# Layer 0's modulations through weight slots on TensorE, residuals spread over three feed-forward groups, a third weight slot, final gathers by pairs of tiles

## The chip, the core and the metric

The kernel runs on one core of one Trainium2 chip. The metric is the device time of one execution in microseconds (us). The core has engines that work side by side, each through its own instructions in order: TensorE (PE, matmuls; PEld is its weight load), VectorE (DVE), ScalarE (ACT), GpSimd (POOL) and SyncE (SP), which here issues most DMAs. Data lies in HBM, in SBUF (128 partitions) and, for matmul results, in PSUM. TensorE's clock has two levels, and the profile gives the granted clock as a share of full speed.

## What is computed

The reference is a two-layer network on 512 tokens `x` and 256 context tokens `ctx`, width 1024, all in fp32. Its main loop, cut:

```python
for l in range(DEPTH):                                   # DEPTH = 2
    mod_x = (cond_x @ w_ada[l] + b_ada[l]).reshape(bsz, 6, 1, d)
    mod_c = (cond_c @ w_ada[l] + b_ada[l]).reshape(6, 1, d)
    hx = x * (1.0 + mod_x[:, 1]) + mod_x[:, 0]
    ...
    x = _layer_norm(DEEPNORM_ALPHA * x + mod_x[:, 2] * mix_x, ln_g[l, 0], ln_b[l, 0])
    hx = x * (1.0 + mod_x[:, 4]) + mod_x[:, 3]
    f_x = _channel_mix(hx, l, ...)      # l = 0: SwiGLU, 2816 wide; l = 1: 8 experts, 2 chosen
    x = _layer_norm(DEEPNORM_ALPHA * x + mod_x[:, 5] * f_x, ln_g[l, 1], ln_b[l, 1])
```

`ctx` goes the same way in layer 0 with `mod_c`. The mix is a projection by `w_in`, two recurrent branches in both directions (HGRN2 and mLSTM), gates and a projection by `w_out`. A modulation m of a layer (m = 0 to 5) is thus a row of 1024 numbers for each of the two streams: a product of `cond` (2 by 1024) with 1024 by 1024 of `w_ada`, 4 MB in HBM.

## The kernel before

**Products.** fp32 products are made of three passes (`mm3`, L166 to L168): each operand is split in a high part and the rest. A weight comes by DMA into a raw buffer `wr` (512 KB, two of them); ACT copies it to `wh` (L133, L150) and DVE subtracts into `wl` (L134, L151). A pair `wh`/`wl` of 128x2048 each is a weight slot. There are two, taken in turn by `load_w` and `load_pair`, so one set of weights is prepared while TensorE works on the other. In a steady stretch TensorE never waits.

**Modulations.** Three forms exist. `ada` (L276) multiplies raw `w_ada` by `cond` on TensorE in plain fp32, 2x512 of output, eight matmuls for a half of a modulation; each raw buffer holds two of them. Layer 0 does m = 1 and 0 so at the start and m = 2 in the mix. `ada_vec` multiplies on the vector engines: for each of 8 k it loads 128x1024 of `w_ada` and adds it, scaled by one column of `cond` for each stream, to an accumulator `acc` (L324 and L326 on DVE; with `both=True` the second stream goes over ACT, L320, and POOL, L322). Its `end` splits `acc` (ACT L332, DVE L333) and sums over the partitions by four or eight short matmuls with the constant `esel` (L338). Layer 0 does m = 4 and m = 3 so with `both=True`, from the gates to the middle of `w_out`; m = 5 and the six of layer 1 go by `ada_vec` in the first seven groups of the feed-forward, from `between`. `ada_put` adds the bias and turns the row.

**Stages in the trace (us).** 0 to 47 start and m = 1, 0; 50 to 505 mix of layer 0 (m = 2 at 203 to 252; the last HGRN heads and gates with m = 4 at 390 to 505); 505 to 620 `w_out`, norm and split of the rows (m = 3); 620 to 1225 feed-forward; 1225 to 1590 mix of layer 1; 1590 to 1660 `w_out` and router; 1660 to 2220 experts; 2226 to 2269 last gathers, norm and output.

**Feed-forward (`swiglu`).** Eleven groups of 256 hidden columns; for each, gate and up products block by block (`b`) and, in a block, for the 512 tokens and the 256 of the context (`spans`), then the down product of all six token tiles in two halves, evacuated by `evac` on DVE (L1015). After group `GRES` = 8, DVE multiplies each half by the modulation row `bd` (L1018) and adds the residual (L1019), which `residual` brings from HBM and POOL scales (L909, L910). The last down pass takes two groups.

**End of layer 1.** `finish` normalises rows (POOL's `pow`, L841; DVE L892), writes them to `xhd`; the router runs on DVE; POOL gathers the first experts' tokens (L1203, indirect DMA); SP loads a register with the first expert's number (`TENSOR_LOAD expi`) and then the experts' weights. In the midst of the experts, `rest` loads the rows `xhd` as `xrows` and scales them on POOL by eight 128x1024 operations (L1450, L1451). At the end eight indirect DMAs (L1529) add the experts' results to the four tiles of `xrows`, first j = 0 for all four tiles, then j = 1; each tile is then normed (L831, L838, L841, L1541, L1542) and written.

**Order.** Each engine's order is fixed when the program is built, by a scheduler that goes by priorities and readiness; SP's queue too is in order, so a DMA that waits holds up those behind it.

Of the kernel before, what the change touches and what calls it, by code (L numbers as in the profile page):

```python
# [17 lines left out]
KT = 8  # L18
# [31 lines left out]
class Kern:  # L50
# [47 lines left out]
    def raw(self, w, own=None):  # L98
        if own is not None:
            return own[0].tile([P, 1024], F32, tag="ar", name=self.nm("ar"), bufs=own[1])[:, :w]  # L100
# [4 lines left out]
    def load_w(self, shape, src, scale=None, own=None):  # L105
# [5 lines left out]
        if own is None:  # L111
            wp, wb = self.wps[self.wi % len(self.wps)]
            self.wi += 1
            h, lo = (wp.tile([P, 2048], F32R, tag=x, name=self.nm(x), bufs=wb) for x in ("wh", "wl"))
        else:
            h, lo = (self.ow.tile([P, 1548], F32R, tag="early", name=self.nm("a"), bufs=2) for _ in range(2))
# [3 lines left out]
        for i, j in parts:  # L120
            w = shape[1] * (j - i)
            r = self.raw(w, own)
# [14 lines left out]
    def load_pair(self, n, src):  # L137
# [4 lines left out]
        for k0 in range(0, KT, kp):  # L142
            wp, wb = self.wps[self.wi % len(self.wps)]
            self.wi += 1
            h, lo = (wp.tile([P, 2048], F32R, tag=x, name=self.nm(x), bufs=wb) for x in ("wh", "wl"))
# [132 lines left out]

    def ada_put(self, l, m, half, pr, ns):
# [16 lines left out]
    def ada_vec(self, l, ms, pool, ns=2, both=False, tmp=None):  # L296

# [3 lines left out]
        if isinstance(ms, int):  # L301
            ms = ((ms, 0), (ms, 1))
        w = self.I["w_ada"][l].rearrange("(k p) c -> k p c", p=P)
        c0 = [m * D + half * 512 for m, half in ms]
        acc = [self.ow.tile([P, 1548], F32, tag="early", name=self.nm("acc"), bufs=2) for _ in range(ns)]
        for k in range(KT):
            wk = self.raw(1024, (pool, 2) if pool else None)
            if c0[1] == c0[0] + 512:
                nc.sync.dma_start(wk, w[k][:, c0[0]:c0[0] + D])
            else:  # L310
                for h in range(2):
                    nc.sync.dma_start(wk[:, 512 * h:512 * h + 512], w[k][:, c0[h]:c0[h] + 512])
            for s in range(ns):
                cs = self.cond32[:, k, s:s + 1]
                o = acc[s][:, :D]
                if both and s:
                    for h in range(2):
                        c = slice(512 * h, 512 * h + 512)
                        t = o[:, c] if k == 0 else acc[h][:, D:D + 512]
                        nc.scalar.activation(t, wk[:, c], AF.Copy, scale=cs)  # L320
                        if k:
                            nc.gpsimd.tensor_tensor(o[:, c], o[:, c], t, OP.add)  # L322
                elif k == 0:
                    nc.vector.tensor_scalar(o, wk, cs, None, op0=OP.mult)  # L324
                else:
                    nc.vector.scalar_tensor_tensor(o, wk, cs, o, op0=OP.mult, op1=OP.add)  # L326

        def end():
            for i in range(ns):
                h, lo = ((tmp or self.lp).tile([P, D], F32R, tag="xn", name=self.nm("xn"), bufs=2) for _ in range(2))  # L330
                o = acc[i][:, :D]
                nc.scalar.activation(h, o, AF.Copy)  # L332
                nc.vector.tensor_tensor(lo, o, h.bitcast(F32), OP.subtract)  # L333
                if i == 0:
                    prs = [self.psum("g", [ns, 512]) for _ in range(2)]
# [4 lines left out]
            for (m, half), pr in zip(ms, prs):  # L340
                self.ada_put(l, m, half, pr, ns)
# [1279 lines left out]
```

## Time and profile before

| | |
|---|---|
| median of 3 runs | 2271.22 us (2268.95 to 2277.7) |
| profiled execution | 2271.0 us, of it span 2269.2 us and 1.8 us around it |
| busy in the span | PE 2060.2 us (91%), DVE 1511.8 (67%), ACT 914.4 (40%), POOL 255.6 (11%) |
| instructions | 31798 |
| HBM | 305.98 MB read, 22.09 MB written |

The busy time is a mean over stages. The rows further below are read stage by stage: how long PE is busy in a stretch, at which clock, and what ended the idle time ahead of an instruction. Matmuls are pipelined, so a record's length is longer than what one adds to a dense row of them.

### The profile page before, as it was taken

The page shows a single profiled execution, that of the slowest core. Times are in us where ns is not written, and L with a number is a line of the kernel's source. Part 1 is how long each engine was busy: PE and PEld are TensorE (multiplying, and loading weights), DVE is VectorE, ACT ScalarE, POOL GpSimd, SP SyncE. Part 2 cuts the span into 40 slices and gives each one's busy share as a digit, 9 for nine tenths or more (in the row PEclk, how much of TensorE's full clock was granted, in tenths as well). Part 3 has the DMA queues.
Part 4 walks back from the last instruction along what each step waited for, and adds up shares of the span by engine and source line. Part 5 has one row for each costly group of instructions (what it writes and reads, how often), then busy time and mean ns, then how long its engine had stood idle before and what let it go on. Part 6 is the DMA issues. An engine that isn't in the chain of part 4 may idle for free. (4 is left out here: it accounts for less than half of the span.)

```text
span 2269.2 us, 31798 instructions
## 1 busy us (share of the span) xinstructions
PE 2060.2 (91%) x12225; PEld 1753.9 (77%) x12225; DVE 1511.8 (67%) x2527; ACT 914.4 (40%) x1447; POOL 255.6 (11%) x211
## 2 busy tenths in 40 slices
PE   8999899897899999999699999999869999897991
PEld 4886788896788788888588888899867787675771
DVE  4465776857866774334727577686679768778774
ACT  3345333343432222212124354334247656665661
POOL 1001101414300000000400001111310000004003
PEclk9999999998899999999899999999869999899995
DMA  7122302246543662112222222124368779887875
GB/s 261 40 89 89 93 27 63 63 138 206 192 153 127 197 208 71 56 56 65 84 66 85 58 83 66 47 61 141 135 196 302 255 242 317 269 271 262 289 272 126
DMA packets 231493, 330.21 MB, mean 146 GB/s; under 512 B 14512, under 2 KB 181620, under 8 KB 231336
## 3 DMA queue, kind: packets, MB, share of 16 engines
q1 hardware_dynamic: 227928, 317.04, 43.2%
q0 software_dynamic: 3408, 11.08, 1.9%
q8 instruction: 98, 1.61, 0.3%
q14 instruction: 59, 0.48, 0.1%
HBM read 305.98 MB, written 22.09 MB: 145 GB/s over the span
## 5 line engine op out<-in xcount | busy, mean ns | idle before, releaser
L168 PE MATMUL g<-xh,wl 128*128 128x512 f32 (+1 forms) x1168 | 402.4, 345 | 15.8 <-DVE wl L134 15.8
L166 PE MATMUL g<-xh,wh 128*128 128x512 f32 (+1 forms) x1168 | 402.5, 345 | 2.5 <-ACT wh L133 2.0
L167 PE MATMUL g<-xl,wh 128*128 128x512 f32 (+1 forms) x1168 | 401.8, 344 | 1.9 <-DVE xl L385 1.9
L134 DVE TENSOR_TENSOR wl<-wr,wh 128x1024 fp32r<-128x1024 f32 x240 | 296.2, 1247 | 139.3 <-ACT wh L133 131.1
L133 ACT ACTIVATE wh<-wr 128x1024 fp32r<-128x1024 f32 x240 | 249.3, 1055 | 244.5 <-PE sc L168 72.8
L166 PE MATMUL g<-wh,xh 128*128 128x256 f32 x1024 | 298.2, 292 | 15.0 <-DVE pre L975 6.6
L167 PE MATMUL g<-wl,xh 128*128 128x256 f32 x1024 | 298.8, 292 | 8.4 <-DVE wl L130 5.8
L168 PE MATMUL g<-wh,xl 128*128 128x256 f32 x1024 | 296.8, 290 | 0.0
L168 PEld LDWEIGHTS g<-xh,wl 128*128 128x128 f32 x1168 | 221.4, 190 | 43.6 <-DVE wl L134 17.1
L166 PEld LDWEIGHTS g<-xh,wh 128*128 128x128 f32 x1168 | 221.7, 190 | 30.3 <-ACT wh L133 2.9
L167 PEld LDWEIGHTS g<-xl,wh 128*128 128x128 f32 x1168 | 221.2, 189 | 29.5 <-DVE xl L385 2.4
L151 DVE TENSOR_TENSOR wl<-wr,wh 128x1024 fp32r<-128x1024 f32 x154 | 191.2, 1251 | 50.6 <-ACT wh L150 49.6
L166 PEld LDWEIGHTS g<-wh,xh 128*128 128x128 f32 x1024 | 198.5, 194 | 20.2 <-DVE pre L975 6.9
L167 PEld LDWEIGHTS g<-wl,xh 128*128 128x128 f32 x1024 | 198.4, 194 | 11.8 <-DVE wl L130 8.0
L168 PEld LDWEIGHTS g<-wh,xl 128*128 128x128 f32 x1024 | 198.6, 194 | 0.8 <-issue 0.8
L150 ACT ACTIVATE wh<-wr 128x1024 fp32r<-128x1024 f32 x154 | 161.6, 1056 | 75.8 <-DMA wr<-in_moe_w_gate_up 64.3
L326 DVE SCALAR_TENSOR_TENSOR acc<-ar,cond,acc 128x1024 f32<-128x1024 f32 x77 | 101.3, 1330 | 35.3 <-DMA ar<-in_w_ada 35.3
L864 DVE TENSOR_TENSOR s<-g,s 128x512 f32<-128x512 f32 (+1 forms) x44 | 24.4, 555 | 146.9 <-PE g L168 146.9
L524 POOL TENSOR_TENSOR ss<-ss,mhalf 128x4 f32<-128x4 f32 (+1 forms) x22 | 27.2, 1237 | 666.9 <-DVE ss L523 499.0
L865 ACT ACTIVATE hh<-s 128x512 fp32r<-128x512 f32 (+1 forms) x44 | 23.0, 523 | 174.2 <-DVE s L864 174.2
L467 PE MATMUL sc<-tmp,s 128*128 128x128 f32 x560 | 79.6, 290 | 9.7 <-DVE tmp L475 7.4
L909 POOL TENSOR_TENSOR xr<-xr,gbc 128x512 f32<-128x512 f32 x20 | 31.0, 1552 | 484.1 <-DMA xr<-xd 476.5
(483 smaller groups left out, 4164.7 us busy)
## 6 DMA issues: line engine op xcount, KB each, us to landing
wr<-in_moe_w_gate_up SPq DMA_DIRECT2D x176, 512.0 KB
wr<-in_moe_w_down SPq DMA_DIRECT2D x88, 512.0 KB
wr<-in_w_in SPq DMA_DIRECT2D x64, 512.0 KB
ar<-in_w_ada SPq DMA_DIRECT2D x64, 512.0 KB
wr<-in_ffn_w_gate_up SPq DMA_DIRECT2D x44, 512.0 KB
wr<-in_w_ada SPq DMA_DIRECT2D x32, 512.0 KB
wr<-in_ffn_w_down SPq DMA_DIRECT2D x22, 512.0 KB
wr<-in_w_out SPq DMA_DIRECT2D x16, 512.0 KB
```

The lines of the kernel that those rows point to most:

```text
L133: nc.scalar.activation(fl(h), r, AF.Copy)
L134: nc.vector.tensor_tensor(fl(lo), r, fl(h).bitcast(F32), OP.subtract)
L150: nc.scalar.activation(v(h, u), r, AF.Copy)
L151: nc.vector.tensor_tensor(v(lo, u), r, v(h, u).bitcast(F32), OP.subtract)
L166: nc.tensor.matmul(out, ah, bh, start=(i == 0), stop=False)
L167: nc.tensor.matmul(out, ah, bl, start=False, stop=False)
L168: nc.tensor.matmul(out, al, bh, start=False, stop=(i == n - 1))
L326: nc.vector.scalar_tensor_tensor(o, wk, cs, o, op0=OP.mult, op1=OP.add)
L467: nc.tensor.matmul(pl[:, c - a], kc[:, c * P:(c + 1) * P], apx(qa, c * P + T, [[2 * hh, 64 // hh], [hh - T, 2], [1, hh]]), start=True, sto ...
L524: nc.gpsimd.tensor_tensor(ss[:, :n], ss[:, :n], self.mhalf[:, :n], OP.pow)
L864: nc.vector.tensor_tensor(s, pu, s, OP.mult)
L909: nc.gpsimd.tensor_tensor(xr, xr, gb[0][:, c], OP.mult)
```

## The change

1. `ada_slot` is new: a half of a modulation (2 MB of `w_ada`) is loaded by two 1 MB DMAs straight into a weight slot, `wh` and `wl` both taken as plain fp32 space, and its eight matmuls with `cond` come when the returned `end` is called. Layer 0's m = 2 goes so (one half ahead of each `wq` load), m = 4 (one half in each of the last two gates) and m = 3 (one half in each of the first two quarters of `w_out`, in the third slot).
2. A third weight slot (`wh3`, `wl3`) takes: the two halves of m = 3, the last quarter of layer 0's `w_out`, the loads of `ada_vec` in the feed-forward (m = 5 of layer 0 and layer 1's six; four 1 MB DMAs for a modulation in place of eight of 512 KB, and `h`, `lo` of its end in the slot too), and the first weights of the last down pass.
3. In the feed-forward's first group the 512 tokens of both blocks come ahead of the context's 256.
4. `GRES` becomes a function of the tile: tiles 0, 1 take their residual after group 6, 2, 3 after 7, and 4, 5 after 8; a tile's later down products are multiplied by `bd` one by one. The residual rows are prepared one group ahead.
5. After layer 1's last `pow`, POOL scales `pre` by `ln_g`, `ln_b` (eight 128x1024 operations) and SP writes it to `xd`; `xrows` in the experts is loaded from there and its eight POOL operations go.
6. The final gathers go by pairs of tiles: j = 0 and 1 of tiles 0, 1, then of 2, 3.

```diff
+    def ada_slot(self, l, m, half, third=False):
+        ws = [t.bitcast(F32).rearrange("p (k c) -> p k c", c=512) for t in self.wslot(third)]
+        for i, t in enumerate(ws):
+            nc.sync.dma_start(t, w[:, 4 * i:4 * i + 4, c0:c0 + 512])
+        def end():
+            pr = self.psum("g", [2, 512])
+            for k in range(KT):
+                nc.tensor.matmul(pr, self.cond32[:, k], ws[k // 4][:, k % 4], start=k == 0, stop=k == KT - 1)
+            self.ada_put(l, m, half, pr, 2)
+        return end
...
+    def ada_vec(self, l, m, ns):
+        for k0 in range(0, KT, 4):
+            for i, t in enumerate(self.wslot(True)):
+                wk = t.bitcast(F32).rearrange("p (k c) -> p k c", c=D)
+                k1 = k0 + 2 * i
+                nc.sync.dma_start(wk, w[:, k1:k1 + 2, m * D:m * D + D])
...
-            if pr == 0:
-                if l == 0:
-                    self.ada(0, (2,))
+            if l == 0:
+                end = self.ada_slot(0, 2, pr)
...
             wq = self.w_cols(w, O_HQ + 256 * pr, 256)
+            if l == 0:
+                end()
...
-            if l == 0 and g == 1:
-                self.ends = [self.ada_vec(0, 4, None, both=True)]
+            if l == 0 and g > 1:
+                end = self.ada_slot(0, 4, g - 2)
...
-            for b in range(nb):
-                for t0, n in spans:
+            for b, (t0, n) in ([(b, s) for s in spans for b in range(nb)] if g == 0 else itertools.product(range(nb), spans)):
...
-                dh, dl = self.load_w((nb, D), lambda i, j: dv[:, i:j])
+                dh, dl = self.load_w((nb, D), lambda i, j: dv[:, i:j], third=g == len(groups) - 1 and not ps)
...
-                                  scale=lambda k: self.norm_col(l, k)) for nq in nqs]
+                                  scale=lambda k: self.norm_col(l, k), third=nq == 3 and not last) for nq in nqs]
+                if l == 0 and nqs[0] < 2:
+                    end = self.ada_slot(0, 3, nqs[0], True)
...
             if last:
+                with tc.issue_after(self.pow.ins if hasattr(self.pow, "ins") else self.pow):
+                    for t in range(nt):
+                        for g, op in zip(gn, (OP.mult, OP.add)):
+                            nc.gpsimd.tensor_tensor(pre[:, t], pre[:, t], g, op)
+                        nc.sync.dma_start(self.xd[t * P:(t + 1) * P], pre[:, t])
...
-                if end:
-                    m = self.lp.tile([P, 512], F32, tag="xr", name=self.nm("xm"), bufs=4)
+                if g > GRES(t):
+                    m = self.fp.tile([P, 512], F32, tag="s", name=self.nm("xm"), bufs=2)
                     nc.vector.tensor_tensor(m, p, bd, OP.mult)
                     nc.vector.tensor_tensor(o, o, m, OP.add)
-                    return
-                nc.vector.tensor_tensor(o, p, o, OP.add)
-                if g == GRES:
+                else:
+                    nc.vector.tensor_tensor(o, p, o, OP.add)
+                if g == GRES(t):
                     nc.vector.tensor_tensor(o, o, bd, OP.mult)
-                    nc.vector.tensor_tensor(o, o, self.residual(t, half, gb), OP.add)
+                    nc.vector.tensor_tensor(o, o, res.pop((t, half)), OP.add)
+                if (t, half) == (nt - 1, 1):
+                    for u in tiles:
+                        if GRES(u) == g + 1:
+                            res.update({(u, h): self.residual(u, h, gb) for h in range(2)})
...
-                nc.sync.dma_start(x, xhd.rearrange("(t p) c -> p t c", p=P))
+                nc.sync.dma_start(x, self.xd[0:TX].rearrange("(t p) c -> p t c", p=P))
...
-                for t in range(NX):
-                    nc.gpsimd.tensor_tensor(x[:, t], x[:, t], g1, OP.mult)
-                    nc.gpsimd.tensor_tensor(x[:, t], x[:, t], b1, OP.add)
...
-        for j in range(2):
-            for t in range(NX):
+        for u in range(0, NX, 2):
+            for j, t in itertools.product(range(2), (u, u + 1)):
...
-GRES = D_FF // 256 - 3
+def GRES(t):
+    return D_FF // 256 - 3 - (NT - 1 - t) // 2
```

**Where it moves instructions.** On DVE, in the down pass of group 8 before: `bd` is the modulation row, `xr` a residual, `wl` the next group's weights.

```order
L1015 TENSOR_TENSOR pre_4488<-sc_9159,pre_4488 128x512
L1019 TENSOR_TENSOR pre_4488<-pre_4488,xr_9154 128x512
L1018 TENSOR_TENSOR pre_4488<-pre_4488,bd_5585 128x512
L1015 TENSOR_TENSOR pre_4488<-o_9173,pre_4488 128x512
L1019 TENSOR_TENSOR pre_4488<-pre_4488,xr_9168 128x512
L1018 TENSOR_TENSOR pre_4488<-pre_4488,bd_5585 128x512
L1015 TENSOR_TENSOR pre_4488<-sc_9187,pre_4488 128x512
L1019 TENSOR_TENSOR pre_4488<-pre_4488,xr_9182 128x512
L1018 TENSOR_TENSOR pre_4488<-pre_4488,bd_5585 128x512
L134 TENSOR_TENSOR wl_9202<-wr_9203,wh_9201 128x1024
```

The weights of the next group stand behind all twelve halves, of three operations each. The changed kernel's DVE in the pass of group 7, its middle one:

```order
L1020 TENSOR_TENSOR xm_8576<-sc_8569,bd_5480 128x512
L135 TENSOR_TENSOR wl_8688<-wr_8689,wh_8687 128x1024
L1021 TENSOR_TENSOR pre_4468<-pre_4468,xm_8576 128x512
L1020 TENSOR_TENSOR xm_8586<-o_8579,bd_5480 128x512
L1020 TENSOR_TENSOR xm_8596<-sc_8589,bd_5480 128x512
L1021 TENSOR_TENSOR pre_4468<-pre_4468,xm_8586 128x512
L1021 TENSOR_TENSOR pre_4468<-pre_4468,xm_8596 128x512
L1023 TENSOR_TENSOR pre_4468<-o_8599,pre_4468 128x512
L1023 TENSOR_TENSOR pre_4468<-sc_8609,pre_4468 128x512
L1025 TENSOR_TENSOR pre_4468<-pre_4468,bd_5480 128x512 x2
L1026 TENSOR_TENSOR pre_4468<-pre_4468,xr_8291 128x512
L1026 TENSOR_TENSOR pre_4468<-pre_4468,xr_8295 128x512
```

One quarter of the next weights (`wl_8688`) has moved among the evacuations; the other three stand behind the pass as before.

On POOL, at the end of layer 1's norm, before (`r` is `pow`, `gat` the first experts' gathers):

```order
L841 TENSOR_TENSOR r_13934<-r_13934,mhalf 128x1
L841 TENSOR_TENSOR r_14025<-r_14025,mhalf 128x1
L1203 DMA gat_14217<-xhd,ix_0_14187 128x1024
L1203 DMA gat_14219<-xhd,ix_1_14198 128x1024
L1203 DMA gat_14222<-xhd,ix_0_14209 64x1024
```

and in the changed kernel at the same place:

```order
L843 TENSOR_TENSOR r_13798<-r_13798,mhalf 128x1
L843 TENSOR_TENSOR r_13889<-r_13889,mhalf 128x1
L997 TENSOR_TENSOR pre_13256<-pre_13256,ln_g_1704_13265 128x1024 x2
L997 TENSOR_TENSOR pre_13256<-pre_13256,ln_b_1705_13267 128x1024 x2
L997 TENSOR_TENSOR pre_13256<-pre_13256,ln_g_1704_13265 128x1024
L997 TENSOR_TENSOR pre_13256<-pre_13256,ln_b_1705_13267 128x1024
L997 TENSOR_TENSOR pre_13256<-pre_13256,ln_g_1704_13265 128x1024
L997 TENSOR_TENSOR pre_13256<-pre_13256,ln_b_1705_13267 128x1024
L1215 DMA gat_14093<-xhd,ix_0_14063 128x1024
L1215 DMA gat_14095<-xhd,ix_1_14074 128x1024
L1215 DMA gat_14098<-xhd,ix_0_14085 64x1024
```

Eight 128x1024 operations have come between `pow` and the first gather. SP's queue at the same place, before (`expi` is the first expert's number, `wr` its weights):

```order
L894 DMA xhd<-pre_13398 128x1024 x4
L1428 TENSOR_LOAD expi
L1428 ISA x2
L123 ISA
L123 DMA wr_14500<-in_moe_w_gate_up 128x4x256
```

and in the changed kernel:

```order
L998 DMA xd<-pre_13256 128x1024 x4
L1440 TENSOR_LOAD expi
L1440 ISA x2
L124 ISA
L124 DMA wr_14376<-in_moe_w_gate_up 128x4x256
```

Four writes to `xd`, each behind POOL's operations on its tile, have come between the writes to `xhd` and the register load with the experts' first weights.

## Rows read from the trace of the kernel before

**Rows 1.** The page's first part: TensorE's busy time over the span.

```profile
PE 2060.2 (91%) x12225; PEld 1753.9 (77%) x12225; DVE 1511.8 (67%) x2527; ACT 914.4 (40%) x1447; POOL 255.6 (11%) x211
```

**Rows 2.** Busy time by stretch: columns named in the first line, x = records.

```profile
core 0: us, PE busy (x) PEld busy (x) DVE busy (x) ACT busy (x) POOL busy (x), PEclk, DMA share, GB/s
0.00:50.00 50.00, 41.84 (x152) 16.07 (x153) 20.57 (x61) 14.29 (x30) 6.98 (x23) 0.97 0.79 275
...
203.00:252.00 49.00, 38.94 (x168) 20.81 (x168) 26.22 (x63) 17.73 (x29) 4.34 (x4) 0.86 0.46 139
410.00:460.00 50.00, 40.65 (x309) 38.43 (x308) 48.10 (x55) 22.69 (x41) 25.74 (x18) 0.97 0.29 83
505.00:600.00 95.00, 80.32 (x604) 75.09 (x603) 79.59 (x127) 36.58 (x69) 31.96 (x22) 0.91 0.58 189
600.00:625.00 25.00, 15.13 (x78) 13.04 (x78) 21.41 (x34) 14.65 (x32) 10.83 (x9) 0.73 0.54 189
...
900.00:950.00 50.00, 50.00 (x266) 42.02 (x265) 21.88 (x35) 11.04 (x15) 0.00 (x0) 1.00 0.20 64
1085.00:1118.00 33.00, 14.06 (x47) 10.14 (x46) 29.84 (x27) 1.06 (x1) 24.86 (x16) 0.74 0.25 78
1220.00:1235.00 15.00, 12.04 (x95) 11.04 (x93) 13.49 (x24) 10.98 (x25) 0.55 (x1) 1.00 0.42 108
...
2047.00:2104.00 57.00, 44.46 (x185) 33.26 (x183) 51.69 (x47) 34.09 (x45) 26.32 (x8) 0.97 0.77 253
2104.00:2154.00 50.00, 49.34 (x227) 39.92 (x228) 35.21 (x43) 29.36 (x40) 0.00 (x0) 1.00 0.86 286
```

**Rows 3.** What TensorE waited for: us in total, times, longest.

```profile
PE g L168 <- DVE wl L134: 16.6, 3, 15.4
PE sc L371 <- DVE pre L892: 8.8, 2, 7.9
PE sc L467 <- DVE tmp L475: 7.4, 8, 3.1
...
PE g L338 <- ACT xn L332: 7.0, 2, 5.4
PE g L276 <- DMA wr<-in_w_ada: 6.9, 3, 3.1
```

**Rows 4.** Timeline of TensorE in the first loads of m = 2.

```profile
216.59 2.72 PE L276 MATMUL g<-wr,cond 128*2 128x512 f32 x3 [3.05 <-DMA wr<-in_w_ada]
```

**Rows 5.** The instructions of line 338: duration in ns, min/median/max.

```profile
L338 PE MATMUL g<-xn,esel x56: 387/397/628, 518.1 to 974.8; 128*2 128x512 f32 x40, 128*1 128x512 f32 x16
```

**Rows 6.** Groups by line: busy us, mean ns | idle before, releaser.

```profile
L326 DVE SCALAR_TENSOR_TENSOR acc<-ar,cond,acc 128x1024 f32<-128x1024 f32 x77 | 101.3, 1330 | 35.3 <-DMA ar<-in_w_ada 35.3
...
L322 POOL TENSOR_TENSOR acc<-acc 128x512 f32<-128x512 f32 x14 | 23.5, 1682 | 0.8 <-ACT acc L320 0.8
```

**Rows 7.** The same view of VectorE from 1085 to 1118 us.

```profile
L1018 DVE TENSOR_TENSOR pre<-pre,bd 128x512 f32<-128x512 f32 x8 | 14.1, 1757 | 0.0
L1019 DVE TENSOR_TENSOR pre<-pre,xr 128x512 f32<-128x512 f32 x9 | 9.9, 1104 | 0.0
...
L1015 DVE TENSOR_TENSOR pre<-sc,pre 128x512 f32<-128x512 f32 x4 | 2.7, 678 | 0.0
```

**Rows 8.** Timeline of POOL between layer 1's last pow and the first gather.

```profile
1657.36 1.08 POOL L1203 DMA_INDIRECT gat<-xhd,ix  x1 [18.21 <-DVE oh L1166]
```

**Rows 9.** The instructions of line 1450: duration in ns, min/median/max.

```profile
L1450 POOL TENSOR_TENSOR xrows<-xrows,gat x4: 2398/3090/3976, 2047.6 to 2064.0; 128x1024 f32<-128x1024 f32 x4
```

**Rows 10.** Groups by line, VectorE: one row of 2047 to 2104, one of 2104 to 2180.

```profile
L151 DVE TENSOR_TENSOR wl<-wr,wh 128x1024 fp32r<-128x1024 f32 x18 | 26.7, 1496 | 3.6 <-ACT wh L150 3.4
...
L151 DVE TENSOR_TENSOR wl<-wr,wh 128x1024 fp32r<-128x1024 f32 x27 | 32.8, 1220 | 8.4 <-ACT wh L150 8.1
```

**Rows 11.** The chain that ended last, the pieces of the gathers: start, us, what.

```profile
2230.78 9.44 DMA xrows<-ysd,sidx
...
2240.49 9.69 DMA xrows<-ysd,sidx
```

More of the change, by code (lines that the diff above doesn't have):

```diff
@@ L96, in psum, with wslot, raw @@
         return v
-    def raw(self, w, own=None):
-        if own is not None:
-            return own[0].tile([P, 1024], F32, tag="ar", name=self.nm("ar"), bufs=own[1])[:, :w]
+    def wslot(self, third=False):
+        if third:
+            return tuple(self.lp.tile([P, 2048], F32R, tag=x, name=self.nm(x), bufs=1) for x in ("wh3", "wl3"))
+        wp, wb = self.wps[self.wi % len(self.wps)]
+        self.wi += 1
+        return tuple(wp.tile([P, 2048], F32R, tag=x, name=self.nm(x), bufs=wb) for x in ("wh", "wl"))
+    def raw(self, w):
         wr, rb = self.wrs[self.ri % len(self.wrs)]
@@ L110, in load_w @@
             n *= s
[L111 to L116, printed above, removed]
+        h, lo = self.wslot(third)
         v = lambda t: t[:, :n].rearrange("p (a b) -> p a b", b=shape[1])
@@ L121, in load_w @@
             w = shape[1] * (j - i)
-            r = self.raw(w, own)
+            r = self.raw(w)
             nc.sync.dma_start(r.rearrange("p (a b) -> p a b", b=shape[1]), src(i, j))
@@ L294, in ada_put @@
         nc.vector.tensor_scalar(self.modT[l][:, m, 4 * half:4 * half + 4, :ns], pt, 1.0 if m in (1, 4) else 0.0, None, op0=OP.add)
-    def ada_vec(self, l, ms, pool, ns=2, both=False, tmp=None):
+    def ada_vec(self, l, m, ns):
         nc = self.nc
[L301 to L304, printed above, removed]
+        w = self.I["w_ada"][l].rearrange("(k p) c -> p k c", p=P)
@@ L305, in ada_vec @@
         acc = [self.ow.tile([P, 1548], F32, tag="early", name=self.nm("acc"), bufs=2) for _ in range(ns)]
[L306 to L335, printed above, removed]
-                for j in range(2):
-                    for z, x in enumerate((h, lo)):
-                        nc.tensor.matmul(prs[j], self.esel[:, i, :ns], x[:, j * 512:j * 512 + 512],
-                                         start=(i + z == 0), stop=(i == ns - 1 and z == 1))
-            for (m, half), pr in zip(ms, prs):
-                self.ada_put(l, m, half, pr, ns)
@@ L808, in mix @@
                 nc.scalar.activation(sg[:, t], p, AF.Sigmoid if g < 2 else AF.Silu)
+            if l == 0 and g > 1:
+                end()
             yg.append((c0, sg))
@@ L978, in run @@
                             add_x(t, 0)
-                        if l == 0 and t == (3 if nqs[0] == 0 else 5):
-                            self.ends.pop()()
-                            if nqs[0] == 0:
-                                self.ends.append(self.ada_vec(0, 3, self.lp, both=True))
+                        if l == 0 and t == nt - 1:
+                            end()
                         continue
```

60 lines of the change are left out of this document (38 added, 22 removed).

## The prediction

> **What bounds the kernel now.** I read the page's busy times first, then the stretches, then TensorE's waits, and only then single lines. TensorE is busy for 2060.2 us of 2269.2 [rows 1], and in a plain stretch of the feed-forward for 50.00 of 50 [rows 2]: there only less work for it would help. The other 209 us lie in a few stretches, and those are where this change works: 203 to 252 (modulation m = 2), 410 to 460 and 505 to 600 (m = 4, m = 3), 600 to 625 (start of the feed-forward), 1085 to 1118 (residuals), 1220 to 1235, 2047 to 2104 (rows in the experts) and the tail. From a row of the stretches two numbers follow: the idle time (length less PE busy), and an upper bound of what the lower clock lost. At 0.86 of full speed over 49 us, 2 x 0.14 x 49 = 13.7 us were at the lower of the two levels, which costs at most half of it, 6.9 us. At most, since part of that time TensorE was idle anyway.
>
> One group of the feed-forward has 264 matmuls (96 of 256 tokens, 168 of 512 columns) and the dense row has 266 records in 50 us [rows 2], so one of 512 adds 50 / (168 + 48) = 0.23 us and one of 256 half of that. A weight slot of 256 columns against 768 tokens keeps TensorE for 48 x 0.23 + 48 x 0.115 = 16.6 us; a down pass of 72 takes 16.6 us too.
>
> The sum is made against the profiled execution, 2271.0 us (span 2269.2 and 1.8 around it); the median of the runs, 2271.22, is the same to 0.01%.
>
> **m = 2.** The same 16 matmuls, moved. Idle 10.1 us, of it 6.9 for raw `w_ada` [rows 2, 3], and at most 6.9 for the clock: 17.0 to be had. A half is now one 2 MB load ahead of its use. At the 139 GB/s of this stretch that takes 15.1 us and at the 275 of the first 50 us 7.6 [rows 2]; both lie under the 16.6 us of the slot before it. The next weights are then prepared under the half's own matmuls. I take -13; -7 if only the wait for raw data goes, -17 at best.
>
> **m = 4 and m = 3.** Here TensorE gets work that VectorE, ScalarE and POOL did: 4 halves of 8 matmuls at 2.72 / 3 = 0.91 us [rows 4], 29.0 us. Sixteen short matmuls go; a record has 0.40 us [rows 5], a dense one added 0.23, so 3.7 to 6.4; I take 4. So +25. What it buys: 410 to 460 has 9.4 us idle and at most 1.5 lost to the clock, 505 to 600 has 14.7 and 8.6, together 34. In the first, VectorE is busy for 48.1 of 50 us and POOL for 25.7; TensorE's wait there is for VectorE's `tmp` (7.4 us in all), and in the second for the split of `acc` (7.0) [rows 2, 3]. 14 operations at 1.33 us on VectorE (and two shorter) and 28 of up to 1.7 on POOL go [rows 6], and the new matmuls depend on DMA alone, so that TensorE has work while VectorE catches up. I take 28 of 34 recovered: -3. Ends: only the named waits and half of the rest, 20, is +5; all of it -9.
>
> **Start of the feed-forward.** From 600 to 625 idle 9.9 us, of it 7.9 in one wait for the norm of the last tile, and at most 6.8 for the clock [rows 2, 3]. That tile's latency stays, but with the tokens ahead of the context TensorE has both blocks' 512-token products (96 x 0.23 = 22 us) before it needs the last two tiles, and the third slot sets a weight slot free earlier. m = 5 still stands between the norms on VectorE. I take -9 of 16.6, ends -4 and -16.
>
> **Residuals.** From 1085 to 1118 TensorE is busy for 14.06 of 33 us: 18.9 idle, of it 15.4 in one wait for `wl`, at a clock of 0.74, at most 8.6 more [rows 2, 3]. The wait is VectorE's: twelve halves of 0.68 + 1.76 + 1.10 us [rows 7], 42 us, and then four weights of 1.22. That is 47 against a pass of 16.6, and yet only 18.9 idle: weights made before gave some 12 us of cover. After the change the passes of groups 6, 7 and 8 have 20, 24 and 28 operations (four halves of the three, and two in place of one for each half done before). At 0.68 that is 14, 16 and 19 us, with three weights behind it at most 23; less 16.6 that is 6.4, under the 12 of cover. The rows come one group ahead, so nothing waits for POOL. I take -21 of 27.5; -15 if the last two passes each leave 4 to 6 us. The last down pass has its first weights in the third slot: of 3.0 us idle from 1220 to 1235 [rows 2] I take -2, ends 0 and -3.
>
> **`ada_vec` in the feed-forward.** Seven modulations, as many bytes in half as many DMAs. VectorE waited for them for 35.3 us in all [rows 6], mostly without TensorE noticing. A group moves 3 MB of weights and 4 MB of `w_ada`. For two streams VectorE has 16 x 1.33 = 21 us beside its 21.9 [rows 2, 6], so 7 us of slack in 50. If loads of 1 MB set the pace at 139 GB/s, 30 us for four, VectorE has 52 us of work and waiting in a group: 2 us too much, 14 over seven. At the other end 0. I take +2.
>
> **Rows of layer 1's norm.** POOL's eight operations move from the experts, where they met VectorE, to the router. *There:* 57 - 44.46 = 12.5 us idle and at most 1.7 of clock, with VectorE busy for 51.7 of 57; the next 50 us have 0.7 idle [rows 2]. A weight split took 1.50 us beside POOL and 1.22 without [rows 10]. I take -9, ends -6 and -14. *Here:* POOL was idle for 18.21 us before the first gather at 1657.36, so from 1639.15 [rows 8]. Eight operations of 2.40 (the shortest) to 3.29 us (26.32 / 8) [rows 2, 9] end at 1658.3 to 1665.5. So the gathers, and through SP's four writes the register load and the experts' first weights behind them, start 1 to 8 us later; and the router's operations on VectorE are slowed as the splits were. I take +6, with +1 and +14 as ends: it is nearer to the longer row, since VectorE is at work in this stretch too.
>
> **Tail.** The chain holds 19 us of gathers [rows 11], bound by their own pace, which stays; two tiles are complete one or two gathers earlier, and their norms no longer queue behind the last. -2, ends 0 and -4.
>
> **The sum:** -13 - 3 - 9 - 21 - 2 + 2 - 9 + 6 - 2 = -51, so 2271 - 51 = 2220 us.
>
> **Rivals.**
> *(a) POOL and VectorE block each other in the router.* There the operations of the router's chain read SBUF twice, as the splits do, and each could stand behind a POOL operation of 2.4 to 3.3 us; POOL in turn behind them. Then gathers come at 1665.5 and what is left of the chain, up to 7 us, behind that: +15 in place of +6, 2229. For it: 1.50 against 1.22 us [rows 10]. Against: part of the chain is short and reads PSUM. The Trainium skill (SBUF — State Buffer, section Who interferes with whom) says that a VectorE operation with two SBUF inputs and a GpSimd operation that reads SBUF exclude each other for a whole instruction; by that rule it would be this rival here and the upper end of the gain in the experts there. The rows on the splits agree with it in direction.
> *(b) TensorE pays and the gaps stay.* The slot is free too late, or 2 MB come late; then the change does not do what it says. m = 2 gives 0, m = 4 and m = 3 recover 10 of 34, +15: 0 + 15 - 9 - 21 - 2 + 2 - 9 + 6 - 2 = -20, 2251. Against: 15.1 us of load at the slowest under 16.6 of cover. For: it is close.
> *(c) Slower: the feed-forward starves.* A reload of the third slot waits on SP for VectorE's four operations (5.3 us, twice for a modulation), with the group's weights behind it. If that adds to the 7 MB of a group at 139 GB/s (53 us), a group takes 53 + 10.6 = 64 us in place of 50 and seven lose 95: -53 + 95 = +42, 2313. It decides from 147 GB/s down (7.34 MB in 50 us), and makes the whole slower from 9 us a group. Against: the same bytes came through two smaller buffers, 35.3 us of waiting in all [rows 6].
> *(d) More than the sum:* the clock's losses and the gaps go in full in m = 2, the start and the residuals, 17 + 16 + 27 against the 43 taken: 2203.
>
> **How the numbers follow.** Forecast 0.60 (2208 to 2236 by itself), (a) 0.13, (b) 0.10, (c) 0.06, (d) 0.11. A measurement here can tell some 0.5% (11 us) from no change, so faster means under 2260. Forecast, (a) and (d) lie there, and two thirds of (b); the rest of (b) and mild cases of (c) are within. Faster 0.87, same 0.07, slower 0.06. The range leaves out (c), the far side of (d) and the far side of (b): 2197 to 2252.
>
> **What would show it.** Right: in the changed profile TensorE dense at full clock from 203 to 252; `sc L371 <- pre` under 5 us and `L168 <- wl` under 6; the stretch of the old 2047 to 2104 with POOL empty and under 4 us idle; TensorE's total at 2060 + 25 less what the full clock gives back, 2070 to 2085. Wrong, if plain stretches of the feed-forward fall under 49 of 50 (c), if eight POOL operations end after 1666 by today's clock and the router's take 20% longer (a), or if the new matmuls wait for `in_w_ada` (b).

## The result: half of what was forecast

The changed kernel took 2242.64 us (median of 4 runs, 2239.29 to 2247.36) against 2270.09 us beside it: ratio 0.9891, 95% interval 0.9870 to 0.9911, so 20 to 30 us less. Forecast were 51 us less (2220). The time lies in the stated range, the direction is right, and the size is half. The profiled execution took 2239.3 us, and its span is 31.8 us shorter than that of the kernel before; the accounts below are made between these two executions.

The page of the changed kernel, TensorE's row (lines of this kernel are 0 to 12 off those of before):

```profile
PE 2063.8 (92%) x12273; PEld 1746.0 (78%) x12273; DVE 1467.1 (66%) x2519; ACT 891.3 (40%) x1411; POOL 204.1 (9%) x185
```

TensorE has 48 records more (each of the eight matmuls of a half leaves two: 64 new ones, less the 16 short ones that go) and is busy 3.6 us more than in [rows 1], not 10 to 25; the mean granted clock went from 0.951 to 0.96, so fewer matmuls ran long. The stretches of [rows 2] in the changed kernel (same columns; the last two are behind 30 us of change, so they show other work than before), and at their end the plain stretch:

```profile
203.00:252.00 49.00, 42.52 (x217) 29.73 (x215) 27.16 (x64) 19.21 (x30) 5.87 (x4) 0.91 0.21 66
410.00:460.00 50.00, 48.30 (x398) 47.20 (x398) 37.17 (x65) 17.46 (x32) 5.70 (x5) 1.00 0.11 30
505.00:600.00 95.00, 90.45 (x635) 72.65 (x634) 57.05 (x122) 31.35 (x68) 7.04 (x9) 1.00 0.56 189
600.00:625.00 25.00, 22.16 (x137) 19.49 (x136) 22.34 (x35) 15.28 (x35) 9.67 (x8) 0.93 0.63 223
1085.00:1118.00 33.00, 33.00 (x189) 28.69 (x188) 12.03 (x16) 6.49 (x10) 0.00 (x0) 1.00 0.16 49
2047.00:2104.00 57.00, 54.48 (x251) 43.05 (x250) 43.66 (x53) 37.58 (x52) 0.00 (x0) 1.00 0.87 287
900.00:950.00 50.00, 50.00 (x268) 42.14 (x267) 31.36 (x44) 11.16 (x15) 0.00 (x0) 1.00 0.44 148
```

The stretches are denser, and the plain one is as full as before, so the feed-forward does not starve (rival (c)). But two new places appear where TensorE stands, one just behind the first of these stretches and one in the router. Its waits, the longest first (us in total, times, longest):

```profile
PE sc L453 <- POOL s L787: 12.0, 2, 10.4
PE tr L1125 <- DVE Mc L1123: 8.8, 1, 8.8
PE sc L1183 <- DVE oh L1178: 6.8, 2, 6.4
...
PE sc L370 <- DVE pre L894: 3.2, 2, 2.8
...
PE g L167 <- DVE wl L135: 1.6, 2, 1.1
```

The wait for `wl` that was 16.6 us [rows 3] is 1.6, and the one for the last tile's norm 3.2 instead of 8.8. The first three rows have grown: before, the first pair was 2.8 us in all and the router's two 3.0 and 3.4.

To see where the 31.8 us come from I cut each execution at the same events (starts of the same instructions) and compare the pieces:

| from one event to the next, us | before | changed | halves together | rows back | residual once | both (together, rows back) |
|---|---|---|---|---|---|---|
| start to first gate | 390.1 | 397.5 | 385.5 | 397.9 | 397.9 | 385.3 |
| to `w_out`'s first evacuation | 124.5 | 130.3 | 130.9 | 129.5 | 129.7 | 130.5 |
| to the feed-forward's first gate product | 117.2 | 99.9 | 98.2 | 101.3 | 98.3 | 101.2 |
| to its last gate product | 551.1 | 523.9 | 522.7 | 522.8 | 543.7 | 524.1 |
| to layer 1's last `pow` | 455.7 | 453.6 | 457.8 | 452.9 | 456.4 | 454.5 |
| to the first gather | 18.8 | 29.5 | 29.6 | 16.4 | 29.6 | 18.7 |
| to the experts' last gate product | 558.9 | 550.8 | 547.2 | 558.4 | 553.1 | 554.0 |
| to the end | 52.9 | 51.9 | 53.1 | 53.5 | 52.7 | 52.5 |
| span | 2269.2 | 2237.4 | 2225.0 | 2232.7 | 2261.4 | 2220.8 |

The right four columns are experiments below. Before against changed: +7.4, +5.8, -17.3, -27.2, -2.1, +10.7, -8.1, -1.0.

### The profile page after: what moved, and what is told of

It is laid out like the page before. It is cut to its first block, busy times and chain, and to the rows that moved or that the text cites. A ratio compares the mean times of both kernels' runs of the same rounds, so it can differ in the third digit from the quotient of the medians.

```text
span 2237.4 us, 31754 instructions
## 1 busy us (share of the span) xinstructions
PE 2063.8 (92%) x12273; PEld 1746.0 (78%) x12273; DVE 1467.1 (66%) x2519; ACT 891.3 (40%) x1411; POOL 204.1 (9%) x185
## 5 line engine op out<-in xcount | busy, mean ns | idle before, releaser
L135 DVE TENSOR_TENSOR wl<-wr,wh 128x1024 fp32r<-128x1024 f32 x240 | 295.6, 1241 | 158.3 <-ACT wh L134 157.4
L150 DVE TENSOR_TENSOR wl<-wr,wh 128x1024 fp32r<-128x1024 f32 x154 | 185.6, 1219 | 50.6 <-ACT wh L149 49.0
L523 POOL TENSOR_TENSOR ss<-ss,mhalf 128x4 f32<-128x4 f32 (+1 forms) x22 | 27.2, 1240 | 694.6 <-DVE ss L522 525.3
L466 PEld LDWEIGHTS sc<-tmp,s 128*128 128x128 f32 x560 | 71.6, 193 | 10.8 <-issue 4.4
L461 ACT ACTIVATE s<-slot 128x768 f32<-128x768 f32 (+1 forms) x56 | 44.4, 793 | 82.1 <-DVE slot L472 81.3
```

Source lines behind the costliest of these rows:

```text
L135: nc.vector.tensor_tensor(fl(lo), r, fl(h).bitcast(F32), OP.subtract)
L150: nc.vector.tensor_tensor(v(lo, u), r, v(h, u).bitcast(F32), OP.subtract)
L461: nc.scalar.activation(apx(kc, 0, [[2 * hh, qn // (2 * hh)], [hh, 2], [1, hh]]), apx(ka, 0, [[2 * hh, qn // (2 * hh)], [hh + T, 2], [1, hh ...
L466: nc.tensor.matmul(pl[:, c - a], kc[:, c * P:(c + 1) * P], apx(qa, c * P + T, [[2 * hh, 64 // hh], [hh - T, 2], [1, hh]]), start=True, sto ...
L523: nc.gpsimd.tensor_tensor(ss[:, :n], ss[:, :n], self.mhalf[:, :n], OP.pow)
```

## The experiments

### Where the gain of m = 2 went

The prediction took -13 us there, and the first gate came 7.4 us later. Two things stand out. POOL ends the last mLSTM chunk at the same moment in both kernels; its timeline before

```profile
256.48 1.01 POOL L524 TENSOR_TENSOR ss<-ss,mhalf 128x4 f32<-128x4 f32 x1 [20.15 <-DVE ss L523]
...
258.56 5.11 POOL L789 TENSOR_TENSOR s<-slot 128x768 f32<-128x768 f32 x2
```

and in the changed kernel

```profile
256.43 1.01 POOL L523 TENSOR_TENSOR ss<-ss,mhalf 128x4 f32<-128x4 f32 x1 [18.35 <-DVE ss L522]
...
258.52 5.10 POOL L787 TENSOR_TENSOR s<-slot 128x768 f32<-128x768 f32 x2
```

although TensorE's waits for raw `w_ada` ahead of it (6.9 us) are gone. In their place TensorE waits in the chain itself:

```profile
242.27 1.00 PE L730 MATMUL o<-early,tmp 128*128 128x129 f32 x4 [4.73 <-DVE tmp L722]
261.90 1.43 PE L453 MATMUL sc<-s,s 128*128 128x128 f32 x5 [10.38 <-POOL s L787]
```

So the stretch ends with the serial chain of the mLSTM (VectorE, ScalarE, short matmuls, POOL, which waits 18.35 us for the last chunk), not with TensorE's work. The idle time that I counted was time beside that chain.

**Both halves together.** Edit:

```diff
-            if l == 0:
-                end = self.ada_slot(0, 2, pr)
+            if l == 0 and pr == 0:
+                e0, end = (self.ada_slot(0, 2, h) for h in range(2))
+                e0()
...
-            if l == 0:
+            if l == 0 and pr == 0:
                 end()
```

> The changed kernel with both halves of m = 2 ahead of the first query weights (slots kept, the second half no longer ahead of the second pair of heads). Theory 1, the stretch of m = 2 ends with the last mLSTM head (POOL's scaling at 256.4 us in both kernels), so TensorE's idle time there is free and the half that was moved out is paid in full: POOL's 128x768 sums stay at 258.5, the gates come at 390 in place of 397.5, the whole 7 us shorter, about 2235. Theory 2, TensorE is the bound there too (slot loads and the lower clock cost the time): the sums come up to 7 us later and the whole stays at 2242.

Measured: 2231.08 us (2227.02 to 2232.74), ratio 0.9833 (0.9794 to 0.9873). The first gate came at 385.5, 12.0 us before that of the changed kernel, and POOL's sums at 253.5, 5 us earlier: neither theory had that. Seven of the twelve are the half that is now done beside the chain: from POOL's sums to the first gate it takes 132.0 us instead of 139.0. Of the five, 1.3 lie ahead of the last chunk and 3.6 in it. From the start of VectorE's last products for it to the start of ScalarE's last copies of its result, in the changed kernel

```profile
241.79 1.42 DVE L722 TENSOR_TENSOR tmp<-sc,tmp 128x256 f32<-128x256 f32 x4 [1.12 <-ACT tmp L713]
...
251.14 0.80 ACT L737 ACTIVATE num<-o 128x258 f32<-128x258 f32 x2 [3.39 <-PE o L734]
```

and with the halves together

```profile
240.52 1.42 DVE L722 TENSOR_TENSOR tmp<-sc,tmp 128x256 f32<-128x256 f32 x4 [1.12 <-ACT tmp L713]
...
246.30 0.67 ACT L737 ACTIVATE num<-o 128x258 f32<-128x258 f32 x2 [1.75 <-PE o L734]
```

9.4 us against 5.8. The stretch from 203 to 252 has a granted clock of 0.91 in the changed kernel and of 1.00 with the halves together, and the chunk's own matmuls, the same in the same order, take 9.26 us in the one and 5.35 in the other (their windows, with the halves together first):

```profile
203.00:252.00 49.00, 44.60 (x230) 27.78 (x228) 30.61 (x70) 20.97 (x32) 5.86 (x5) 1.00 0.35 108
241.05:246.40 5.35, 5.35 (x33) 4.12 (x33) 0.89 (x3) 0.88 (x3) 0.00 (x0) 1.00 0.00 0
```

```profile
242.27:251.53 9.26, 9.25 (x32) 6.88 (x32) 0.93 (x3) 1.16 (x3) 0.00 (x0) 0.53 0.00 0
```

The chunk's own matmuls run at half clock after TensorE stood for 4.73 us, and they are on the chain. More matmuls beside the chain made the chain shorter.

**The first half left out.** Edit: no `ada_slot` for the first pair of heads; the second half's product is put twice.

> The changed kernel without the first half's product of m = 2 (the second half's rows stand for both; eight matmuls of 7.3 us and 2 MB of loads less, so the output differs). Theory 1 (the mLSTM chain sets the end of the stretch): POOL's sums stay at 258.5, the gates at 397.5, the whole within 2 us of the changed kernel's. Theory 2 (TensorE's work and its slot loads set it): 7 to 12 us less by 258 us and at the end.

The whole (2347 us) says nothing, since other modulations send the tokens to other experts. Up to the gates it can be read: POOL's sums at 255.6, the first gate at 394.7, so 2.9 us and 2.8 us earlier for 6.9 us of matmuls left out. Nearer to the first theory than to the second, and again not zero. TensorE stood for 11 us instead of 4.7 there, and the chunk's matmuls ran at half clock too:

```profile
241.28:248.32 7.04, 6.50 (x32) 5.45 (x32) 0.94 (x3) 0.66 (x2) 0.00 (x0) 0.50 0.01 2
```

But they came in another order, eight of one kind (L731) and eight of the other (L735), twice, where the changed kernel changes kind after two to six records, and 32 records took 7.0 us instead of 9.3. That makes most of the 2.9, and it is not what the edit was to test. The order was not tried alone.

**The second half left out.** The same, the other way round.

> The changed kernel without the second half's product of m = 2 (the first half's rows stand for both; eight matmuls less ahead of the second pair of heads, so the output and with it the experts' load differ; only the time to the gates counts). Theory 1, the last mLSTM chunk is held up by TensorE at half clock after it stood idle, and the second half is paid on top: POOL's sums stay at 258.5, the gates come 7 us earlier at 390 to 391, 5 later than with both halves together (385.5). Theory 2, the second half's slot loads cost the 5 us too: gates at 385 to 386.

The whole (2585 us, one run) says nothing again. The first gate at 389.5, POOL's sums at 257.6: the first theory. The chunk takes 9.3 us from VectorE's products to ScalarE's copies, as in the changed kernel. One half beside the chain and none later gives 389.5; both halves beside the chain give 385.5. Eight matmuls more, and 4 us less. What they changed is the clock under the last chunk, whose matmuls come in the same order in all three kernels.

### What the residuals gave

```diff
-                if g > GRES(t):
+                if end:
...
+                if g == GRES(5):
+                    nc.vector.tensor_tensor(o, o, bd, OP.mult)
+                    nc.vector.tensor_tensor(o, o, self.residual(t, half, gb), OP.add)
```

> The changed kernel with all residuals after group 8 again, not prepared ahead. Theory 1, the feed-forward's gain of 27 us is the residuals': the feed-forward 20 to 27 us longer, with one wait of 15 us for the next group's weights, the whole at 2262 to 2269. Theory 2, part of it is the third slot and the larger loads of w_ada: the feed-forward only 12 to 18 us longer, 2254 to 2260.

2260.97 us, ratio 0.9958 (0.9936 to 0.9979). The feed-forward took 543.7 us, 19.8 more than in the changed kernel, and the old wait is back:

```profile
PE g L167 <- DVE wl L135: 14.3, 2, 13.8
```

So the residuals are worth 20 us of the 27 in this stage. The other 7.4 are not theirs; in the kernel before, two waits for down weights that end at 763 and 819 us (2.3 and 1.0 us) with the half clock behind one of them, and a longer residual wait (15.4 against 13.8), make up about that.

**Smaller loads of `w_ada`**, for those 7 us:

```diff
-        for k0 in range(0, KT, 4):
+        for k0 in range(0, KT, 2):
             for i, t in enumerate(self.wslot(True)):
...
-                nc.sync.dma_start(wk, w[:, k1:k1 + 2, m * D:m * D + D])
+                nc.sync.dma_start(wk, w[:, k1:k1 + 1, m * D:m * D + D])
```

> The changed kernel with the feed-forward's w_ada loads in two buffers of 512 KB again, in place of two of 1 MB. Theory 1, the larger buffers let VectorE's sums run ahead, so that the down weights are no longer late: the feed-forward 4 to 6 us longer (from 524 to 528 to 530 between its first and last gate evacuation), with TensorE's wait for the down weights back near the second and third group. Theory 2, the 7 us that the residuals do not explain come from the third slot at the ends: no change in that stretch.

2244.41 us, the feed-forward 524.0: no change, so it is not the size of the loads. VectorE did wait more, and the stage was no longer for it; first this kernel, then the changed one (busy, mean ns | idle before, releaser):

```profile
L329 DVE SCALAR_TENSOR_TENSOR acc<-wl,cond,acc 128x1024 f32<-128x1024 f32 x40 | 51.6, 1308 | 27.0 <-DMA wl<-in_w_ada 26.8
```

```profile
L329 DVE SCALAR_TENSOR_TENSOR acc<-wl,cond,acc 128x1024 f32<-128x1024 f32 x40 | 50.5, 1280 | 8.5 <-DMA wl<-in_w_ada 8.0
```

**The last down pass without the third slot** (`third=` dropped in `swiglu`):

> The changed kernel with the last down pass's first weights in one of the two ordinary slots. Theory: TensorE waits 2 to 3 us for the weights of layer 1 after it, so the stretch from the last gate evacuation to layer 1's first POOL sums is 210 to 211 us in place of 208.3, the whole 1 to 3 us longer. Rival: that wait is a matter of VectorE's end of the norm, 208 to 209.

2237.41 us. From the last gate product to layer 1's first POOL sums 209.2 us, against 208.3 in the changed kernel; but the kernels with other edits elsewhere have 208.2 to 210.1 there. Inconclusive: this part is worth 1 us or nothing.

**The old order in the first group** (each block's tokens, then its context):

> The changed kernel with the feed-forward's first group in the old order (each block's tokens, then its context). Theory 1, the new order covers the last tiles' norm and split: the first evacuation 4 to 8 us after where it is relative to the last norm's first pow (from 44.5 us after it to 48 to 52), the whole 4 to 8 us longer. Theory 2, the stretch is shorter since m = 3's and m = 5's operations left the norms on VectorE: less than 2 us.

2243.25 us, and between `w_out`'s first evacuation and the first gate product 100.4 us against 99.9: the second theory. The order of tokens and context gave nothing. What is left as a reason lies on VectorE and POOL, and it was not tried alone. The sums of m = 3 among `w_out`'s evacuations are gone. Between the first and the last of the six norms (579.82 to 618.50 before, 583.81 to 615.38 in the changed kernel) VectorE had eight sums of m = 5 and now has none: their loads go to the third slot, which `w_out`'s last quarter holds. And three of the six scalings took 1.75 to 1.78 us before, each beside an operation of POOL on residual rows, where the others took 0.81; in the changed kernel all six take 0.81. The kernel before, VectorE and then POOL:

```profile
579.82 0.81 DVE L892 TENSOR_SCALAR pre<-pre,mv,r 128x1024 f32<-128x1024 f32 x1 [0.47 <-POOL r L841]
...
592.56 1.78 DVE L892 TENSOR_SCALAR pre<-pre,mv,r 128x1024 f32<-128x1024 f32 x1 [0.45 <-POOL r L841]
```

```profile
592.49 1.29 POOL L909 TENSOR_TENSOR xr<-xr,gbc 128x512 f32<-128x512 f32 x1
```

### The router

VectorE's timeline between layer 1's last norm and the first experts, before (start, us, the operation, what ended the idle time ahead):

```profile
1639.18 0.81 DVE L892 TENSOR_SCALAR pre<-pre,mv,r 128x1024 f32<-128x1024 f32 x1 [0.41 <-POOL r L841]
...
1649.66 0.15 DVE L1579 TENSOR_TENSOR rte<-mx 128x4 f32<-128x4 f32 x1
...
1649.99 0.29 DVE L1575 TENSOR_TENSOR O<-iota,xfi 128x32 f32<-128x32 f32 x2
1650.32 0.19 DVE L1108 TENSOR_TENSOR M<-O 128x32 f32<-128x32 f32 x1
```

and in the changed kernel, with POOL's last row operation below it:

```profile
1605.77 2.82 DVE L894 TENSOR_SCALAR pre<-pre,mv,r 128x1024 f32<-128x1024 f32 x1 [0.41 <-POOL r L843]
...
1618.27 1.89 DVE L1584 TENSOR_TENSOR rte<-mx 128x4 f32<-128x4 f32 x1
...
1620.27 2.31 DVE L1580 TENSOR_TENSOR O<-iota,xfi 128x32 f32<-128x32 f32 x2
1622.62 2.29 DVE L1120 TENSOR_TENSOR M<-O 128x32 f32<-128x32 f32 x1
```

```profile
1622.52 2.34 POOL L997 TENSOR_TENSOR pre<-pre,ln_b 128x1024 f32<-128x1024 f32 x1
...
1634.73 1.07 POOL L1215 DMA_INDIRECT gat<-xhd,ix  x1 [9.87 <-DVE oh L1178]
```

Operations of 0.15 to 0.3 us take 1.9 to 2.3, as long as what is left of POOL's operation of 2.34; three of them lose 5.9 us and the norm 2.0. POOL itself is done 9.87 us before the gather: its queue holds up nothing. Nor do SP's four writes: the first expert's weights are issued 3.8 us ahead of the first gather, where before they were issued 2.6 us behind it (1657.36 [rows 8]). SP's queue before, then in the changed kernel:

```profile
1659.99 4.38 SPq L123 DMA_DIRECT2D wr<-in_moe_w_gate_up  x4
```

```profile
1630.92 2.52 SPq L124 DMA_DIRECT2D wr<-in_moe_w_gate_up  x4
```

The rest, some 3 us, is VectorE's order: from the counts (L1116, L1128) to the first `oh` it now does first a row of operations of 0.2 to 0.4 us that stood behind before (expert numbers, capacities, slots, the tokens' weights), 1626.92 to 1632.88, against 1652.53 to 1655.52 before.

**Rows back among the experts** (point 5 of the change undone):

> The changed kernel with the scaling of layer 1's rows put back among the experts, as before. Theory 1, POOL's eight operations hold up VectorE's two-input operations in the router (1.9 to 2.3 us for operations of 0.15 to 0.3) and cost 8 to 11 us there, more than the 7 they save among the experts: first gather 11 us nearer to the last norm (18 us after the last pow in place of 29), experts 6 to 7 us longer, the whole 2 to 5 us shorter. Theory 2, the experts' gain is larger than the router's loss: the whole 3 to 8 us longer.

2233.72 us (2228.58 to 2240.64), ratio 0.9844 (0.9798 to 0.9889): the first theory, with 8.9 us less in the whole where it had 2 to 5. The first gather followed the last `pow` by 16.4 us, and the experts took 558.4. Over all kernels: with the rows in the router the gather follows by 29.5 or 29.6 in eight of them, and without by 16.4 to 18.8 in three, so they cost 11.5 us there by the means (10.7 to 13.2). The experts take 543.7 to 556.7 in the eight kernels that scale no rows in them and route alike (mean 550.7) and 554.0 to 558.9 in the three that do (mean 557.1): 6 us, within a scatter of 13. By these stages point 5 loses about 5 us; by the medians of the whole, the two pairs of kernels that differ in it alone (the changed one and this one; the halves together, without and with this edit) give 8.9 and 8.3.

**Half of the row operations.** `zip(gn[:1], (OP.mult,))`: four operations instead of eight.

> The changed kernel with four of POOL's eight row operations (the multiplications stay, the additions are left out, so the output differs, the routing not). Theory 1, the loss in the router is the hold-up of VectorE's two-input operations while POOL works: POOL is done at about 1615 before the router's chain begins, the three operations of 1.9 to 2.3 us fall back to 0.15 to 0.3, and the first gather follows the last pow by 23 to 24 us in place of 29.5; what is left over the 16.4 without row operations is the long norm (2 us) and VectorE's changed order (3) and the like. Theory 2, it is all VectorE's changed order and SP's queue: 28 to 30 us.

23.7 us from the last `pow` to the first gather, as the first theory has it. POOL is done before the router's chain begins, and the three operations are short again:

```profile
1604.99 9.72 POOL L997 TENSOR_TENSOR pre<-pre,ln_g 128x1024 f32<-128x1024 f32 x4
```

```profile
1617.54 0.14 DVE L1584 TENSOR_TENSOR rte<-mx 128x4 f32<-128x4 f32 x1
1617.87 0.29 DVE L1580 TENSOR_TENSOR O<-iota,xfi 128x32 f32<-128x32 f32 x2
1618.20 0.19 DVE L1120 TENSOR_TENSOR M<-O 128x32 f32<-128x32 f32 x1
```

5.8 of the 11.5 us are thus the three operations' wait. The norm's scaling, still behind a POOL operation (2.82 us), is 2, and the rest fits VectorE's order; neither was tried alone. The whole stayed at 2242.45, since the experts happened to take 556.7.

### Better than both

**Halves together and rows back:**

> Both halves of m = 2 together and the scaling of the rows back among the experts, the rest as changed. If the two effects lie in stages of their own they add: 12 us (gates 397.5 to 385.5) and 4 us (end after the last pow 632 to 628 us) off the changed kernel's 2242, about 2226, ratio 0.980 to 0.983 to the kernel before. If the earlier expert stage is bound by weight loads and takes the gain back, 2230 to 2234.

2222.77 us (2220.51 to 2223.98), ratio 0.9792 (0.9764 to 0.9820): 47 us under the kernel before and 20 under the changed one. The effects lie in stages of their own and add, as the last column of the table shows.

**Halves together and the rows early**, each tile's as soon as it is normed (no `issue_after`):

> Both halves of m = 2 together, and POOL's row operations let go as soon as each tile is normed, in place of all behind the last pow. Theory 1 (POOL's hold-up of VectorE is the cost in the router): POOL has three operations left after the last pow (7 us, done before the router's chain begins 12 us after it), so the first gather follows the last pow by 22 to 24 us in place of 29.5, the experts keep their gain, the whole 4 to 7 us under the 2231 of the kernel with the halves together, if layer 1's w_out does not grow by as much. Rival: the operations hold up VectorE's evacuations in w_out instead, which takes 3 to 6 us more, and nothing is won: 2229 to 2233.

2230.66 us (2228.42 to 2234.24), ratio 0.9828 (0.9799 to 0.9858): the rival's time, though not by its mechanism, since VectorE's evacuations (L980) kept their 0.42 us. The gather came 23.8 us after the last `pow`, 6 less, but layer 1 up to that `pow` took 460.9 us against 454.5 and 457.8. The last `pow` now stands behind a row operation, and the norm behind both; POOL, then VectorE:

```profile
1596.02 2.34 POOL L997 TENSOR_TENSOR pre<-pre,ln_g 128x1024 f32<-128x1024 f32 x1
1598.31 0.55 POOL L844 TENSOR_TENSOR r<-r,mhalf 128x1 f32<-128x1 f32 x1
```

```profile
1598.90 2.82 DVE L895 TENSOR_SCALAR pre<-pre,mv,r 128x1024 f32<-128x1024 f32 x1 [4.84 <-POOL r L844]
```

## Where the prediction was right and where not

**m = 2: the step that failed.** Forecast -13, measured +7.4; the 20 us between them are the whole miss, since the others cancel to 1 us. The prediction turned TensorE's idle time into time gained, because each gap had a releaser (raw `w_ada`) that the change takes away. The step left out was to ask what is next once that releaser is gone. The answer was in the trace of before: POOL waited 20.15 us for VectorE up to 256.48, and TensorE's matmuls of the chunk followed VectorE's. Even with both halves kept in the stretch the gate comes only 4.6 us earlier than before (385.5 against 390.1), and the chain itself accounts for that: the last chunk took 9.7 us before, with its matmuls at half clock,

```profile
241.72:250.27 8.55, 8.55 (x37) 6.91 (x35) 2.67 (x3) 1.86 (x4) 0.00 (x0) 0.50 0.48 129
```

and 5.8 with the halves together. Nor did the prediction see that the half which moved out of this stretch goes to one where TensorE is the bound (7.1 of the 8.0 us that leaving it out gave lie behind POOL's sums), nor that the chain's own matmuls would still run at half clock (5 us; with the 7 the 12 of the first experiment). None of the rivals had this: (b) put it down to late loads, and there were none.

**m = 4 and m = 3, and the start of the feed-forward: right in sum, in part by luck.** Forecast -3 - 9 = -12, measured +5.8 - 17.3 = -11.5; the two pieces are not cut where the two terms are, so only the sum can be compared. The reason given for the second was wrong: the order of tokens and context, taken as its cover, changes nothing, and m = 5, which was to stay between the norms, does not stand there any more. That is what is left as a reason, not shown. The price of the new matmuls was luck too: 2.72 / 3 = 0.91 us [rows 4] is the length of a record at half clock, and a matmul leaves two. The stretch of that row in the kernel before, and a half of m = 2 at full clock in the changed one:

```profile
216.60:219.90 3.30, 3.30 (x4) 0.46 (x5) 3.22 (x10) 0.64 (x2) 1.19 (x2) 0.50 0.45 168
```

```profile
360.87 3.59 PE L290 MATMUL g<-wh,cond 128*2 128x512 f32 x8
364.30 3.60 PE L290 MATMUL g<-wl,cond 128*2 128x512 f32 x8
```

The two misreadings cancel: a half takes 6.9 us, where 8 x 0.91 = 7.3 were taken. And the term's upper end, +5, does not follow from its words: the named waits, 14.4 us, and half of the other 19.6 are 24 us, which is +1.

**Residuals: right.** Forecast -21, measured -19.8 by the experiment, with the mechanism named: VectorE's chain ahead of the next group's weights.

**`ada_vec`: mis-sized.** Forecast +2, measured about -7 for all that is not the residuals. It is not the size of the loads. What else removed the two waits for down weights (the place of m = 5's sums, the end's buffers) was not tried and stays open.

**Row operations: rival (a).** Forecast +6 in the router and -9 among the experts; measured +10.7 and -8.1 between the two profiles, +11.5 and -6 over all kernels. The half of (a) in which VectorE stands behind POOL is shown row by row; the other, POOL held up behind VectorE, is not: by the clock of before its eight operations ended at 1658.3, the early end of the forecast. The price lies between the forecast's and its +15. The sum went by POOL's queue and took the slowing of VectorE from a long operation (1.50 against 1.22 us), where the addition is 0.3 us. Here short ones lost more than that, 1.7 to 2.1 us each, and a router is made of short ones. The trace of before had such a price too: 0.81 us became 1.78 for the norm's scaling in layer 0, beside POOL's 1.29. The Trainium skill (SBUF — State Buffer, section Who interferes with whom) states that a VectorE operation with two SBUF inputs and a GpSimd operation that reads SBUF exclude each other for the whole instruction, and that VectorE's scalar operations can do so too in a mode that uses both ports. The trace agrees with both: 0.15 us became 1.89 for two SBUF inputs, and 0.81 became 2.82 for the norm's scaling, which has one. Operations from PSUM beside them kept their length (the four scalings of a norm tile's half, 1.36 and 1.37 us before, 1.35 and 1.37 after).

**Last down pass and tail.** Forecast -2 each; 0 to -2 and -1.0.

**The sum.** The misses are +20.4 (m = 2), +4.7 and +0.9 (rows), -9.4 (`ada_vec`), and +2.6 for the rest: -51 becomes -32, the two profiles' difference. The check named for it, TensorE dense at full clock from 203 to 252, failed plainly (0.91); those on the waits for `wl` and for the norm came out as written. TensorE's total missed its range (2063.8 against 2070 to 2085). In the experts POOL is empty, but the same work, some 30 us earlier now, still has 5.1 us idle instead of under 4:

```profile
2017.00:2074.00 57.00, 51.91 (x227) 40.70 (x226) 45.41 (x57) 38.35 (x55) 0.00 (x0) 0.97 0.89 298
```

## What to carry to other kernels

Idle time of the main engine is worth something only if no other chain ends at the same moment: after taking away the releaser of a gap, follow back the next thing that the engine waits for, and look whether its time moves. Here, matmuls that depend on DMA alone shortened the serial chain beside them, by keeping the clock up under the chain's own matmuls; the same work moved to a dense stretch was paid in full. POOL's long operations cost more beside a chain of short operations on VectorE (11.5 us) than among the experts (some 6, within a scatter of 13).

## What the runs showed of the hardware

- A VectorE operation of 0.15 us with two SBUF inputs took 1.89 us, and two of 0.15 in a row 2.31, beside POOL's 128x1024 operations of 2.34 us; a 128x1024 scaling with one SBUF input took 2.82 instead of 0.81, started 0.07 us after a POOL operation.
- After TensorE had stood for 4.73 us the granted clock fell to half, and the last mLSTM chunk took 9.4 us from VectorE's products to ScalarE's copies instead of 5.8 at full clock. Its 32 records of matmuls took 9.26 us at half clock where the two kinds alternate, and 7.04 in blocks of eight.
- A plain fp32 matmul of two output rows and 512 columns left two records: 16 in 6.9 us for a half at full clock, and a record began 0.81 to 0.86 us after the one before at half clock, 0.43 at full.
- POOL's 128x1024 operation with two SBUF inputs took 2.34 us in the router, most of the eight, where the same operations among the experts took 3.29 on average.
